# Triangular inversion of the gated delta rule: whole 128 x 128 weights in its products, and a new sequence of pieces

## The chip, the cores and the metric

The kernel runs on one core of a Trainium2 chip. The metric is the device time of one execution in microseconds (us). The engines are PE (TensorE), DVE (VectorE), ACT (ScalarE), POOL (GpSimd) and SP (SyncE, which issues the DMAs).

## The reference, cut to what matters

A two-layer encoder (512 tokens of width 1024). Each layer makes one wide projection; a differential attention with four heads and a gated delta rule with four heads, run in both directions, work on its parts; their results are gated, added and projected, and an MLP follows. The change touches the delta rule alone: the inverse of `eye + L`, where `L` is strictly lower triangular within chunks of 64 tokens. The kernel works it out in blocks of its own of 128 tokens.

```python
def gated_delta_rule_chunked(q, k, v, g, beta):
    ...
    L = jnp.where(strict, jnp.einsum('bhncd,bhnmd->bhncm', kb, k) * decay, 0.0)
    eye = jnp.eye(CHUNK, dtype=jnp.float32)
    T = lax.linalg.triangular_solve(eye + L, jnp.broadcast_to(eye, L.shape), left_side=True,
                                    lower=True, unit_diagonal=True)
    u = jnp.einsum('bhncm,bhnme->bhnce', T, v * beta[..., None])
    w = jnp.einsum('bhncm,bhnmd->bhncd', T, kb * jnp.exp(g)[..., None])
    ...
    def step(state, inp):
        ...
def reference(x, c, ada_w, ...):
    for l in range(DEPTH):
        ...
        proj = h @ w_in[l]
        ...
        y_a = diff_attention(...)
        y_b = gated_deltanet(...)
        ...
        x = x + gt1 * (merged @ w_out[l])
        h = rms_norm(x, norm2_g[l]) * (1.0 + sc2) + sh2
        x = x + gt2 * (jnp.square(jax.nn.relu(h @ w_mlp1[l])) @ w_mlp2[l])
    return x
```

## The kernel before

Python code first builds a list of operations, then a planner (`Plan.schedule`) sets the order in which every engine issues them, and `Plan.issue` (L431) emits them; so all rows of the profile name L431, and a group is known by its tiles. The planner is a list scheduler: it keeps a clock for every engine, gives each operation the time that `cost` (L451 and on) states, adds the lag between two engines from `LAG`, and takes at each step, of the operations that are ready, the one with the lowest key. The key is a level and the place in the program. `HOLD` lets a dense product wait for a moment when an operation of a more urgent level is about to be ready. Tiles come from pools of slots (F, Y, Z, and the eight PSUM banks B), and an operation can start only when its slot is free. Where the cost of an operation changes, the place of all later ones can change with it.

Dense products (`d_dn`, `d_da`, `d_z`, `d_g`, `d_out`, `d_m`) are done in a split form: each weight and each activation is a high part and a low part in the fp32r type (`whi`, `wlo`, `hh`, `hl`), and three products are added. ACT casts the high part of a weight, DVE subtracts to get the low part, and both come from a DMA.

`ORDER` (L490) is one string per layer and sets the order in which the pieces stand in the program: `q`, `k`, `v` are the projections of the attention, `d` the projection of a head of the delta rule (`d_dn`, with convolution and norm on DVE), `a` its first part (`kk`, `L`, `kq`, transposes `tokT` and `qT`), `b` the inversion of all 32 x 32 diagonal blocks at once on DVE (`gdn_b`, one batch for four heads), `z` a gate projection, `c` the rest of a head (`gdn_c`), and `t` a head of the attention. The digits are heads, or halves for `q`, `k` and `v`.

`gdn_c` (L1058 and on) joins the inverted diagonal blocks to the inverse of a whole 128 x 128 triangle, for four token tiles (`t`) and both directions (`d`). `four` issues four matmuls into one bank. First `pn` = `L` times the diagonal blocks, copied by ACT or DVE to `NTr`; then three products `px` = `NTr` times a part of `X`, one block diagonal after the other (`n` = 1, 2, 3), and each result is added or copied into `X` before the next one reads it. So `pn`, `px`, `px`, `px` of a direction are a serial chain through PE and ACT or DVE, and the serial recurrence over tokens (`pv`, `R`, `Vk`, `pS`) follows. In the kernel before, the stationary operand of a product has only the columns that the result needs: 128 or 96 for `pn` and for `n` = 1, 64 for `n` = 2 and 32 for `n` = 3. These operands are plain F32, and each such matmul stands in the profile as two instructions, each with its own weight load.

Of the kernel before, what the change touches and what calls it, by code (L numbers as in the profile page):

```python
# [17 lines left out]
P = 128  # L18
# [12 lines left out]
NB = 32  # L31
# [419 lines left out]
def cost(eng, fn, dst, ins, kw):  # L451
    n = int(np.prod(dst.shape[1:]))
    ptr = sum(isinstance(kw.get(k), View) for k in ("scalar", "scalar1", "scale", "bias"))
    psum = any(v.t.cls == "B" for v in ins)
    if ins:
        n = max([n] + [int(np.prod(v.shape[1:])) for v in ins]) if eng != "pe" else n
    if eng == "sp":
        return int(np.prod(dst.shape)) * 4 / 360.0
    if eng == "pe":
        if fn == "transpose":  # L460
            return 109.0
        if kw["lhsT"].dt == F32:
            return 4 * max(n, 32) / 2.4 + 9.0
        return 120.0 if n <= 256 else n / 2.4 + 14.0
    if eng == "act":
        return (51.0 if psum else 93.0) + 93.0 * ptr + n / 1.2 + (93.0 if kw.get("accum_out") is not None else 0.0)
    if eng == "dve":
        if fn == "memset":
            return 8.0 + n / 0.96
        if fn == "reciprocal":  # L470
            return 69.0 + 6.25 * n
        return 69.0 + 60.0 * ptr + n / 0.96
    if fn == "memset":
        return 36.0 + n / 1.2
    return 150.0 + (1.66 if any(v.a.strides[-1] == 0 for v in ins) else 2.1) * n
# [11 lines left out]
GS, NYF, KEEPM = (3, 5), 2, (3, 2)  # L487


ORDER = ("q0 d0 a0 d1 a1 d2 a2 d3 a3 b0 k0 z0 c0 z1 c1 k1 z2 q1 v0 t0 z3 t1 c3 c2 v1 t2 t3",  # L490
         "d0 q0 k0 d1 a1 d2 a0 a2 d3 a3 b0 z0 c0 z1 c1 k1 z2 c2 v0 t0 q1 z3 v1 c3 t2 t3 t1")


@with_exitstack
def encoder(ctx, tc, a, out):
# [3 lines left out]
    pe, act, dve, pool, sp = (Eng(pl, e) for e in ("pe", "act", "dve", "pool", "sp"))  # L499
    ad, dp = Eng(pl, "act", "dve"), Eng(pl, "dve", "pool")  # L500
# [126 lines left out]
    for i in range(2):  # L627
        half = slice(512 * i, 512 * i + 512)
        ps = B([P, 512], "cps")
# [143 lines left out]
    for l in range(DEPTH):  # L773
# [9 lines left out]
        for w in range(2):  # L783
            pool.tensor_tensor(out=cg[:, w], in0=ccos, in1=bc(gain[:, l, w], 1, NT), op=ALU.mult, after=[normed])
            pool.tensor_tensor(out=sg[:, w, :, 0:32], in0=csin[:, :, 0:32], in1=bc(gain[:, l, w, 32:64], 1, NT), op=ALU.mult,
                               after=[normed])
            pool.tensor_tensor(out=sg[:, w, :, 32:64], in0=csin[:, :, 32:64], in1=bc(gain[:, l, w, 0:32], 1, NT), op=ALU.mult,
                               after=[normed])
# [269 lines left out]
        def gdn_c(h, XA):  # L1058
# [16 lines left out]
            def four(name, lhsT, rhs, rows, cs):  # L1075
                ps = B([P, NT, P], name)
                for t in range(NT):
                    op = pe.matmul(ps[rows, t, cs], lhsT=lhsT[:, t], rhs=rhs[:, t], start=True, stop=True)
                return ps[rows, :, cs], op

            for d in range(2):
                NTr = Y([P, NT, P], "NT")
                if d == 0:
                    c1, full, ks = slice(0, P - NB), slice(0, P), slice(0, P)
                else:
                    c1, full, ks = slice(NB, P), slice(0, P - NB), slice(0, P - NB)
                    pool.memset(NTr[ks, :, 0:NB], 0.0, after=[gate["inv"]])
                ps, gate["pq"] = four("pn", L[:, d, :, full], DT[:, d, :, c1], full, c1)  # L1090
                ad.copy(NTr[full, :, c1], ps)
                for n in range(1, 4):
                    m = P - NB * n
                    rows, cs = (slice(0, m), slice(NB * n, P)) if d == 0 else (slice(0 if n == 1 else P - m, P), slice(0, m))
                    ps, op = four("px", NTr[ks, :, rows], X[ks, d, :, cs], rows, cs)
                    x = X[rows, d, :, cs]
                    if n == 1:
                        dve.tensor_tensor(out=x, in0=ps, in1=x, op=ALU.add)
                    else:
                        ad.copy(x, ps)  # L1100
# [453 lines left out]
```

## Time and profile before

| | us |
|---|---|
| median of 3 runs (1634.34 to 1637.26) | 1635.57 |
| profiled execution, its own time | 1637.45 |
| its span | 1635.7 |
| PE busy in the span | 1597.4 |
| DVE busy | 1314.3 |
| ACT busy | 829.7 |
| POOL busy | 164.9 |

The granted clock of the span is 0.99 of full speed. In the rows, PE is the matmul side of TensorE and PEld its weight load. A row of the timeline begins with its start and its duration; the name is result <- operands, then the shape of the weight (rows * columns), the shape of the result, and how many instructions in a row have this form. Matmuls are pipelined, so a row lasts longer than its distance to the next one: what an instruction costs is read from the distance between starts.

### The profile page before, as it was taken

To read this page: it belongs to the slowest core of one execution; us is meant where nothing else is said; L and a number is where in the kernel's file an instruction comes from. 1 tells how busy PE (TensorE), PEld (TensorE's weight loads), DVE (VectorE), ACT (ScalarE), POOL (GpSimd) and SP (SyncE) were. 2 spreads that over 40 slices of the span, in tenths; PEclk is the share of its full clock that TensorE was granted. 3 is DMA by queue.
4 is the path that set the end of the run, shared out by engine and by line. 5 is a ranking of instruction groups with operands and counts; after the bars stand their busy time and mean duration, and the time that the engine had idled before them with its cause. 6 is when DMAs were issued, how large, how long until landed. Compare 5 with 4: busy or idle time off the path is not lost.

```text
span 1635.7 us, 25251 instructions
## 1 busy us (share of the span) xinstructions
PE 1597.4 (98%) x9136; PEld 1385.3 (85%) x9136; DVE 1314.3 (80%) x2878; ACT 829.7 (51%) x1591; POOL 164.9 (10%) x170
## 2 busy tenths in 40 slices
PE   6989999999999999999989899999999999999998
PEld 5869988888899888888879799998888988888887
DVE  7999969899899988585998897699527885767676
ACT  4583335573266545454558442467423674636361
POOL 0253201000300000000005221000003000000000
PEclk9989999999999999999989999999999999999999
DMA  9423465538767483436233323422343525252542
GB/s 376 165 75 120 136 221 145 170 116 296 284 251 290 173 303 121 162 122 235 96 129 123 111 90 109 131 69 81 103 142 129 206 91 189 94 191 92 192 168 77
DMA packets 107726, 260.77 MB, mean 159 GB/s; under 512 B 27841, under 2 KB 40769, under 8 KB 107602
## 3 DMA queue, kind: packets, MB, share of 16 engines
q1 hardware_dynamic: 107602, 259.16, 46.1%
q8 instruction: 72, 1.18, 0.3%
q14 instruction: 52, 0.43, 0.1%
HBM read 242.31 MB, written 16.81 MB: 158 GB/s over the span
## 4 chain that ended last, share of the span: by engine, by line
PE 93%; DVE 4%; ACT 1%; issue 0%; DMA 0%; POOL 0%; SPq 0%; DVEq 0%; ACTq 0%
PE d_m L431 19%; PE d_g L431 11%; PE m2x L431 11%; PE d_da L431 8%; PE d_dn L431 6%; PE d_out L431 6%; PE m2y L431 5%; PE d_m1f L431 3%; PE d_z L431 3%; PE m2z L431 3%; PE d_brb L431 3%; PE d_bra L431 3%; PE sc L431 2%; PE px L431 2%; PE po L431 2%; PE pv L431 2%
## 5 line engine op out<-in xcount | busy, mean ns | idle before, releaser
L431 PE MATMUL d_m<-hh,whi_m 128*128 128x512 f32 x448 | 174.5, 389 | 0.0
L431 PE MATMUL d_m<-hl,whi_m 128*128 128x512 f32 x448 | 174.4, 389 | 0.0
L431 PE MATMUL d_m<-hh,wlo_m 128*128 128x512 f32 x448 | 174.4, 389 | 0.0
L431 DVE TENSOR_TENSOR m2lo<-m,m2hi 128x1024 fp32r<-128x1024 f32 x112 | 132.9, 1221 | 13.1 <-ACT m2hi L431 8.6
L431 ACT CAST m2hi<-m 128x1024 fp32r<-128x1024 f32 x112 | 114.8, 1048 | 50.1 <-DMA m<-in_w_m_dram 20.2
L431 DVE SCALAR_TENSOR_TENSOR ada<-ada,cb 128x1024 f32<-128x1024 f32 x96 | 116.5, 1227 | 2.6 <-DMA ada<-in_ada_w_dram 2.6
L431 PE MATMUL d_da<-whi_da,hh 128*128 128x256 f32 x384 | 109.4, 285 | 0.0
L431 PE MATMUL d_da<-whi_da,hl 128*128 128x256 f32 x384 | 109.1, 284 | 0.0
L431 PE MATMUL d_da<-wlo_da,hh 128*128 128x256 f32 x384 | 108.8, 285 | 0.0
L431 ACT ACTIVATE relu<-d_m 128x512 f32<-128x512 f32 x56 | 33.5, 598 | 147.8 <-PE d_m L431 147.8
L431 PE MATMUL d_g<-hh,wlo_g 128*128 128x512 f32 x256 | 102.0, 399 | 0.0
L431 PE MATMUL d_g<-hl,whi_g 128*128 128x512 f32 x256 | 102.0, 399 | 0.0
L431 PE MATMUL d_g<-hh,whi_g 128*128 128x512 f32 x256 | 102.0, 398 | 0.0
L431 PEld LDWEIGHTS d_m<-hh,wlo_m 128*128 128x128 f32 x448 | 84.1, 188 | 17.4
L431 PEld LDWEIGHTS d_m<-hh,whi_m 128*128 128x128 f32 x448 | 84.1, 188 | 17.4
L431 PEld LDWEIGHTS d_m<-hl,whi_m 128*128 128x128 f32 x448 | 84.1, 188 | 17.4
L431 PE MATMUL d_dn<-hh,whi_dn 128*128 128x512 f32 (+1 forms) x208 | 78.4, 387 | 2.6 <-DVE L L431 2.6
L431 PE MATMUL d_dn<-hh,wlo_dn 128*128 128x512 f32 (+1 forms) x208 | 79.3, 385 | 1.6 <-DVE wlo_dn L431 1.6
L431 DVE TENSOR_TENSOR u<-relu 128x256 f32<-128x256 f32 x64 | 27.1, 423 | 66.8 <-ACT relu L431 66.5
L431 PE MATMUL d_dn<-hl,whi_dn 128*128 128x512 f32 (+1 forms) x208 | 80.5, 387 | 0.0
L431 ACT CAST whi_m<-raw_m 128x1024 fp32r<-128x1024 f32 x56 | 58.7, 1049 | 42.3 <-DMA raw_m<-in_w_mlp_dram 35.7
L431 DVE TENSOR_TENSOR wlo_m<-raw_m,whi_m 128x1024 fp32r<-128x1024 f32 x56 | 67.9, 1221 | 12.6 <-ACT whi_m L431 12.4
(326 smaller groups left out, 4777.9 us busy)
## 6 DMA issues: line engine op xcount, KB each, us to landing
m<-in_w_m_dram SPq DMA_DIRECT2D x112, 512.0 KB, 4.3
ada<-in_ada_w_dram SPq DMA_DIRECT2D x96, 512.0 KB, 6.1
raw_m<-in_w_mlp_dram SPq DMA_DIRECT2D x56, 512.0 KB, 4.6
raw_g<-in_w_g_dram SPq DMA_DIRECT2D x32, 512.0 KB, 4.4
raw_out<-in_w_out_dram SPq DMA_DIRECT2D x32, 512.0 KB, 4.3
raw_dn<-in_w_dn_dram SPq DMA_DIRECT2D x24, 512.0 KB, 6.3
raw_da<-in_w_da_dram SPq DMA_DIRECT2D x24, 512.0 KB, 3.9
xs<-xT SPq DMA_DIRECT2D x24, 256.0 KB, 2.5
```

Of the source, the lines that this page charges most:

```text
L431: op.ins = getattr(eng[op.eng[0]], fn)(*[real(v) for v in op.args], **{k: real(v) for k, v in op.kw.items()})
```

## The change

Three things. First, in `gdn_c` all products of `pn` and `px` now take a whole 128 x 128 weight and write all 128 rows of their columns; the same rows as before are copied out of the bank. So that the unused columns of `NTr` are numbers, the 32 columns that `pn` doesn't write are set to zero for both directions and on all 128 rows, where before that was done on 96 rows and for one direction: eight POOL memsets more. The count of matmuls is the same; per layer and head, 4 `pn` go from 96 to 128 weight columns, 4 `px` with `n` = 1 likewise (the other 4 had 128 columns on 96 rows), 8 `px` go from 64 to 128, and 8 from 32 to 128. Second, `cost` gives an F32 matmul at least 111 ns times the share of the 128 result rows, where before at least that of 32 columns. Third, both strings of `ORDER` are new. The shape, the cost and the strings together move instructions all over the program.

```diff
@@ -460,7 +460,7 @@
         if fn == "transpose":
             return 109.0
         if kw["lhsT"].dt == F32:
-            return 4 * max(n, 32) / 2.4 + 9.0
+            return max(4 * n / 2.4 + 9.0, 111.0 * dst.shape[0] / P)
         return 120.0 if n <= 256 else n / 2.4 + 14.0
     if eng == "act":
         return (51.0 if psum else 93.0) + 93.0 * ptr + n / 1.2 + (93.0 if kw.get("accum_out") is not None else 0.0)
@@ -487,8 +487,8 @@
 GS, NYF, KEEPM = (3, 5), 2, (3, 2)
 
 
-ORDER = ("q0 d0 a0 d1 a1 d2 a2 d3 a3 b0 k0 z0 c0 z1 c1 k1 z2 q1 v0 t0 z3 t1 c3 c2 v1 t2 t3",
-         "d0 q0 k0 d1 a1 d2 a0 a2 d3 a3 b0 z0 c0 z1 c1 k1 z2 c2 v0 t0 q1 z3 v1 c3 t2 t3 t1")
+ORDER = ("q0 d0 a0 d1 d2 a1 a2 d3 a3 b0 k0 z0 c0 z1 c1 k1 q1 v0 z2 t0 z3 c2 t1 c3 v1 t2 t3",
+         "d0 q0 d1 k0 a1 d2 a0 a2 d3 a3 b0 z0 c0 z1 c1 v0 k1 z2 c2 t0 q1 v1 z3 t2 t3 t1 c3")
 
 
 @with_exitstack
@@ -1075,24 +1075,22 @@
             def four(name, lhsT, rhs, rows, cs):
                 ps = B([P, NT, P], name)
                 for t in range(NT):
-                    op = pe.matmul(ps[rows, t, cs], lhsT=lhsT[:, t], rhs=rhs[:, t], start=True, stop=True)
+                    op = pe.matmul(ps[:, t, cs], lhsT=lhsT[:, t], rhs=rhs[:, t], start=True, stop=True)
                 return ps[rows, :, cs], op
+
 
 
 
             for d in range(2):
                 NTr = Y([P, NT, P], "NT")
-                if d == 0:
-                    c1, full, ks = slice(0, P - NB), slice(0, P), slice(0, P)
-                else:
-                    c1, full, ks = slice(NB, P), slice(0, P - NB), slice(0, P - NB)
-                    pool.memset(NTr[ks, :, 0:NB], 0.0, after=[gate["inv"]])
-                ps, gate["pq"] = four("pn", L[:, d, :, full], DT[:, d, :, c1], full, c1)
-                ad.copy(NTr[full, :, c1], ps)
+                c1, c0 = (slice(0, P - NB), slice(P - NB, P)) if d == 0 else (slice(NB, P), slice(0, NB))
+                pool.memset(NTr[:, :, c0], 0.0, after=[gate["inv"]])
+                ps, gate["pq"] = four("pn", L[:, d], DT[:, d, :, c1], slice(0, P), c1)
+                ad.copy(NTr[:, :, c1], ps)
                 for n in range(1, 4):
                     m = P - NB * n
                     rows, cs = (slice(0, m), slice(NB * n, P)) if d == 0 else (slice(0 if n == 1 else P - m, P), slice(0, m))
-                    ps, op = four("px", NTr[ks, :, rows], X[ks, d, :, cs], rows, cs)
+                    ps, op = four("px", NTr, X[:, d, :, cs], rows, cs)
                     x = X[rows, d, :, cs]
                     if n == 1:
                         dve.tensor_tensor(out=x, in0=ps, in1=x, op=ALU.add)
```

In the projection stage of the second layer (`ORDER[1]`), PE's rows around the product `kk` of the head that comes first read like this before; `d_dn0`, `d_dn1` and `d_dn2` are the projections of a head's q, k and v, `kk` waits for the k of the head, normed on DVE:

```order
L431 MATMUL d_dn0_9714<-hl7_8915,whi_dn00_9424 128x512
L431 MATMUL d_dn0_9714<-hh7_8911,wlo_dn00_9431 128x512
L431 MATMUL d_dn2_9769<-hh0_8821,whi_dn20_9737 128x512
L431 MATMUL d_dn2_9769<-hl0_8828,whi_dn20_9737 128x512
L431 MATMUL d_dn1_9794<-hh0_8821,whi_dn10_9747 128x512
L431 MATMUL d_dn1_9794<-hl0_8828,whi_dn10_9747 128x512
L431 MATMUL kk_9808<-kqv1_9799 128x128 x4
L431 MATMUL tokT_9819<-cst_86,kqv1_9799 128x128 x4
L431 MATMUL d_dn0_9835<-hh0_8821,whi_dn00_9757 128x512
L431 MATMUL d_dn0_9835<-hl0_8828,whi_dn00_9757 128x512
L431 MATMUL d_dn2_9769<-hh0_8821,wlo_dn20_9829 128x512
L431 MATMUL d_dn2_9769<-hh1_8841,whi_dn20_9737 128x512
```

And now:

```order
L431 MATMUL d_da_9717<-wlo_da100_9433,hh1_8843 128x256
L431 MATMUL d_da_9717<-whi_da100_9424,hh2_8849 128x256
L431 MATMUL d_da_9717<-whi_da100_9424,hl2_8866 128x256
L431 MATMUL d_da_9717<-wlo_da100_9433,hh2_8849 128x256
L431 MATMUL kk_9746<-kqv1_9726 128x128 x3
L431 MATMUL qT_9753<-cst_86,kqv0_9732 128x128 x4
L431 MATMUL kk_9746<-kqv1_9726 128x128
L431 MATMUL kq_9763<-kqv0_9732,kqv1_9726 128x128 x4
L431 MATMUL tokT_9777<-cst_86,kqv1_9726 128x128 x4
L431 MATMUL d_da_9717<-whi_da100_9424,hh3_8872 128x256
L431 MATMUL d_da_9717<-whi_da100_9424,hl3_8881 128x256
L431 MATMUL d_da_9717<-wlo_da100_9433,hh3_8872 128x256
```

The projection `d_da` of the attention's k (`k0`) now stands ahead of `kk`, 49 matmuls in a row, where two starts of `d_dn` of the next head stood; the transposes `qkT` of the attention have left the place.

In `gdn_c` of the head that comes first in the first layer, PE's rows around the first chain read like this before (`px` with the results 96 x 96, 64 x 64 and 32 x 32 are direction 0, the next ones direction 1):

```order
L431 MATMUL px_2646<-X_2554,NT_2626 64x64 x4
L431 MATMUL d_z_2569<-hh5_399,whi_z0_2551 128x512
L431 MATMUL pn_2653<-DT_2423,L_1071 96x96 x3
L431 MATMUL px_2657<-X_2554,NT_2626 32x32 x4
L431 MATMUL pn_2653<-DT_2423,L_1071 96x96
L431 MATMUL d_z_2569<-hl5_406,whi_z0_2551 128x512
L431 MATMUL d_z_2569<-hh5_399,wlo_z0_2596 128x512
L431 MATMUL d_z_2569<-hh6_437,whi_z0_2551 128x512
L431 MATMUL pv_2672<-tok2_942,X_2554 128x128
L431 MATMUL px_2675<-X_2554,NT_2407 128x96 x4
L431 MATMUL d_z_2569<-hl6_446,whi_z0_2551 128x512
L431 MATMUL d_z_2569<-hh6_437,wlo_z0_2596 128x512
```

And now:

```order
L431 MATMUL d_z_2597<-hh7_485,wlo_z0_2592 128x512
L431 MATMUL px_2649<-X_2589,NT_2409 128x64 x4
L431 MATMUL pn_2656<-DT_2425,L_1072 128x96 x4
L431 MATMUL px_2662<-X_2589,NT_2409 128x32 x4
L431 MATMUL px_2678<-X_2589,NT_2412 128x96 x4
L431 MATMUL pv_2684<-tok2_940,X_2589 128x128
L431 MATMUL px_2690<-X_2589,NT_2412 128x64 x4
L431 MATMUL px_2699<-X_2589,NT_2412 128x32 x4
L431 MATMUL pv_2684<-tok2_940,X_2589 128x128
L431 MATMUL pn_2711<-DT_2665,L_1330 128x96
L431 MATMUL pS_2715<-Vk_2707,tok1_641 128x128
L431 MATMUL pn_2711<-DT_2665,L_1330 128x96
```

The gate's dense products `d_z`, which stood between the steps of the chain, are all issued before it reaches its second step; between these steps stand only products of the chain itself and of the recurrence after it, and the next dense product stands 54 rows after the last of them.

## Rows read from the trace of the kernel before

**Rows 1.** The page: busy us and share, and the chain that ended last.

```profile
PE 1597.4 (98%) x9136; PEld 1385.3 (85%) x9136; DVE 1314.3 (80%) x2878; ACT 829.7 (51%) x1591; POOL 164.9 (10%) x170
...
PE 93%; DVE 4%; ACT 1%; issue 0%; DMA 0%; POOL 0%; SPq 0%; DVEq 0%; ACTq 0%
```

**Rows 2.** Windows: stretch, busy us (instructions) by engine, clock, DMA share, GB/s.

```profile
108.00:125.00 17.00, 10.76 (x42) 7.96 (x41) 17.00 (x47) 6.91 (x24) 5.00 (x7) 0.61 0.26 75
896.00:916.00 20.00, 13.09 (x61) 10.85 (x60) 15.76 (x50) 9.57 (x26) 7.22 (x4) 0.83 0.29 84
1010.00:1110.00 100.00, 100.00 (x765) 89.23 (x764) 73.26 (x219) 50.49 (x139) 7.68 (x9) 1.00 0.38 101
```

**Rows 3.** Timeline of PE, blocks of eight F32 instructions between dense products.

```profile
212.98 0.40 PE L431 MATMUL d_z<-hh,whi_z 128*128 128x512 f32 x1
213.21 0.84 PE L431 MATMUL px<-X,NT 128*96 128x96 f32 x8
...
214.15 0.39 PE L431 MATMUL d_z<-hh,wlo_z 128*128 128x512 f32 x1
...
220.09 0.39 PE L431 MATMUL d_z<-hh,wlo_z 128*128 128x512 f32 x1
220.41 0.68 PE L431 MATMUL px<-X,NT 96*64 96x64 f32 x8
...
221.35 0.40 PE L431 MATMUL d_g<-hh,wlo_g 128*128 128x512 f32 x1
...
222.05 0.40 PE L431 MATMUL d_g<-hh,wlo_g 128*128 128x512 f32 x1
222.38 0.44 PE L431 MATMUL px<-X,NT 96*32 96x32 f32 x8
...
223.09 0.40 PE L431 MATMUL d_g<-hl,whi_g 128*128 128x512 f32 x1
...
247.24 0.40 PE L431 MATMUL d_z<-hl,whi_z 128*128 128x512 f32 x1
247.47 1.05 PE L431 MATMUL pog<-V,PT 128*128 128x128 f32 x8
...
248.59 0.60 PE L431 MATMUL pv<-R,X 128*128 128x128 f32 x4
```

**Rows 4.** Timeline of PE, 128 weight columns against 32 moving columns.

```profile
69.94 0.39 PE L431 MATMUL pg<-graw,ones 128*128 128x32 f32 x2
70.16 0.47 PE L431 MATMUL d_dn<-hl,whi_dn 128*128 128x512 f32 x1
```

**Rows 5.** Timeline of PEld, the weight loads of one narrow block.

```profile
220.41 0.54 PEld L431 LDWEIGHTS px<-X,NT 96*64 96x64 f32 x8 [0.36 <-issue]
```

**Rows 6.** Timeline of PE, the waits around the first `kk` of the second layer.

```profile
901.95 1.13 PE L431 MATMUL kk<-kqv 128*128 128x128 f32 x8 [3.65 <-DVE rqr L431]
...
905.58 0.50 PE L431 MATMUL d_dn<-hh,wlo_dn 128*128 128x512 f32 x1 [1.59 <-DVE wlo_dn L431]
...
908.22 0.69 PE L431 MATMUL qkT<-cst,rot 128*128 128x128 f32 x2 [1.67 <-POOL rot L431]
```

**Rows 7.** Timeline of PE, two neighbouring products of the attention's projection.

```profile
885.25 0.28 PE L431 MATMUL d_da<-whi_da,hh 128*128 128x256 f32 x1
885.37 0.28 PE L431 MATMUL d_da<-whi_da,hl 128*128 128x256 f32 x1
```

**Rows 8.** Timeline of PE, the head that comes first, first layer.

```profile
110.11 0.66 PE L431 MATMUL tokT<-cst,kqv 128*128 128x128 f32 x4 [1.74 <-DVE kqv L431]
...
116.48 0.77 PE L431 MATMUL d_dn<-hh,whi_dn 128*128 128x512 f32 x1 [2.61 <-DVE L L431]
...
119.55 1.12 PE L431 MATMUL qT<-cst,kqv 128*128 128x128 f32 x4 [1.87 <-DVE kqv L431]
...
122.03 0.79 PE L431 MATMUL d_dn<-hh,wlo_dn 128*128 128x512 f32 x1
```

**Rows 9.** Timeline of DVE and ACT, results of px going into X.

```profile
214.09 0.55 DVE L431 TENSOR_TENSOR X<-px,X 96x384 f32<-96x384 f32 x1 [0.91 <-PE px L431]
...
215.88 0.36 ACT L431 COPY X<-px 64x256 f32<-64x256 f32 x1 [2.95 <-PE px L431]
```

**Rows 10.** Groups by line, POOL: busy us, mean ns, idle before.

```profile
L431 POOL MEMSET NT<- 96x128 f32 x8 | 1.3, 199 | 0.0
```

## Prediction

> **What bounds the kernel now.** I read the page first: PE is busy in 98% of the span, and it holds 93% of the chain that ended last, DVE 4% [rows 1]. So a change in PE's work shows one for one, except in the few stretches where PE waits. The windows show where these are and where they are not. Between 108 and 125 us PE is busy for 10.76 of 17 us at a granted clock of 0.61, and DVE for all 17; between 896 and 916 us PE is busy for 13.09 of 20 at 0.83. Between 1010 and 1110 us, where the second layer's triangular products lie, PE is busy for 100 of 100 us at 1.00 [rows 2]. So the products that change stand, in the kernel before, in a full PE stream: what they cost is the distance between starts, and nothing hides it. The waits that a new sequence could remove are elsewhere, in the two projection stages.
>
> **Part 1: the whole weights, on PE.** The rows are read as the time from the start of the last dense product ahead of a block of eight instructions (four F32 matmuls) to the start of the second instruction group behind it, so that what a block does to its neighbours is inside. With 128 weight columns that is 248.59 - 247.24 = 1.35 us, with 96 columns 214.15 - 212.98 = 1.17, with 64 columns 221.35 - 220.09 = 1.26, with 32 columns 223.09 - 222.05 = 1.04 [rows 3]. The last three become the first. That the 128-column block has 128 moving columns and the new ones have 96, 64 or 32 makes no difference by the nearest row: two instructions with 128 weight columns against 32 moving ones take 70.16 - 69.94 = 0.22 us, so 0.11 each [rows 4], and the block of eight takes 1.35 less two dense steps of 0.23 (247.47 - 247.24), or 0.89, again 0.11 each [rows 3]. The weight sets the pace, not what moves.
>
> A whole weight therefore costs 0.18 us a block more than 96 columns, 0.09 more than 64, and 0.31 more than 32. The 64-column step is that small because a narrow block pays at its edge: it starts 0.32 us after the dense product ahead of it where the others start 0.23 after [rows 3], and its weight load sits 0.36 us idle before it begins, with no releaser that the profile shows [rows 5]. Per layer and head, direction 0 has one block each of the three kinds (0.58 us); direction 1 has its `pn` with 96 columns, its first `px` already with 128, then one of 64 and one of 32 (0.58 us). Two layers of four heads: 8 x 1.16 = **+9.3 us**. The lower bound is 8.8: the starts are rounded to 0.01, and 48 blocks changed by 0.01 each make 0.5. The upper one is 12.2: some narrow blocks of the kernel before stand next to each other and save the 0.09 at the edge, 32 x 0.09 = 2.9 if all did. I take 9.3, since most have other work between them.
>
> The Trainium skill, page "TensorEngine Tiling (Array Packing)", section "Key Properties", says that a change of the tiling mode drains TensorE. This speaks for the change, as whole weights need no other mode; the 0.36 us of idle weight load agrees with it. By the page alone one would book 32 such drains of 0.36 us as a gain, 11.5 us, and come out at -2.2 us for this part instead of +9.3; the starts in the rows already contain what of them reaches PE's pace.
>
> **Part 2: copies, memsets and the planner's price.** The copies out of PSUM have as many elements in a row as before, so I book nothing. Eight more memsets of about 0.2 us each are 1.6 us on POOL [rows 10], which is busy for 10% [rows 1]; the zeros need no result of the chain, so they lie beside dense work. If that cover were gone, each would hold up one chain by 0.2 us. The new price in `cost` does nothing on the chip but move instructions; that is part 3.
>
> **Part 3: the sequence.** Three places matter.
>
> First, the chain of the first layer. A result of `px` goes to X by DVE in 0.55 us or by ACT in 0.36 [rows 9]. DVE began 0.26 us after the last of the eight starts (213.21 + 7 x 0.089 = 213.83 against 214.09; 0.089 is the 96-column block's 1.17 less 0.46, by eight) [rows 3, 9]. Taking the same 0.26 for the way back, an estimate, the next step of a chain can start 1.07 us (DVE) or 0.88 us (ACT) after that last start, where PE would have gone on after 0.11: 0.96 or 0.77 us of wait. With other work to issue this costs nothing, and before it was there. In the new order the chains of the head that comes first (its direction 1) and of the next head run through 54 rows of PE without a dense product. Step by step, less the work that stands between at 0.11 us an instruction: direction 1 of the first head 0.96 - 0.22 (two instructions of `pv`), 0.77, and 0.5 behind the shortest copy; direction 0 of the next head 0.96 - 0.45 (four instructions) and 0.1 (six); its direction 1 0.96 - 0.45 and 0.77. Together **+3.9 us** of new waits. Bounds: 0 if the recurrence between them happens to fill every gap, and 7 if the recurrence's own steps wait as well. The second half of that layer and the second layer interleave two to four chains, and I book 0 to 1 there.
>
> Second, the start of the second layer's heads. PE waits 3.65 us for DVE's `rqr` ahead of `kk`, 1.59 for the low part of a weight and 1.67 for `rot` [rows 6], 6.9 us in all, and at a clock of 0.83 over 20 us it loses another 3.4 [rows 2]. The new `ORDER[1]` has the k projection of the attention ahead of it: 49 products in a row stand before `kk`, at 0.12 us each [rows 7] 5.9 us. That is more than the longest wait, and may keep the clock up. But the low part of the next weight, which these products need too, comes from DVE, which is busy for 15.76 of the 20 us [rows 2]; in the new order only its high part is used ahead of `kk`, so the planner itself sees it late, and two more waits of 2 us or so remain. I take half of the 10.3 us, **-5 us**; bounds 0 and -10.3.
>
> Third, the start of the first layer's heads. There PE waits 1.74, 2.61 and 1.87 us and takes up its dense stream at 122.03 [rows 8]. DVE is busy in every microsecond [rows 2]. The new `ORDER[0]` lets `d2` go before `a1`, which gives PE other rows to wait with, but the weight's low part, the convolution and `L` are all DVE's, and none gets shorter. What is late next is the same low part. I book **0**, with one such wait either way, -1.9 to +1.9.
>
> **The sum.** 9.3 + 3.9 - 5 + 0 = +8.2 us. The profiled execution took 1637.45 us and would take 1645.6; it is 1.9 above the median, so on the median it is 1635.57 + 8.2 = **1643.8 us**.
>
> **The rivals.** (a) The new sequence pays back the weights: the second layer's waits and slow clock go altogether (-10.3) and the first layer's chain finds its work (0 to +2). That gives -1 to +1, 1635 to 1637. For it: 5.9 us of work against a wait of 3.65. Against it: DVE's 15.76 of 20. (b) Faster: the first layer's start is freed as well. It has 6.2 us of waits and 17 x 0.39 = 6.6 us of clock [rows 2, 8], 12.8 us; with half of that and all of the second layer's the sum is 9.3 + 2 - 10.3 - 6.4 = -5.4, 1630. It decides from the point where the two starts together give back more than the 13.2 us of the weights and the chain; against it stands DVE's full 17 of 17, which no order of PE shortens. (c) Slower still: the 54 rows starve PE so far that the granted clock falls as it did at 108 us. Seventeen microseconds at 0.61 would be 6.6 us more: 1650.4. For it, that gaps of 1.7 to 2.6 us were enough there; against it, that mine are below 1 us each. (d) The page's rule on drains, as a mechanism here: if PE gave back the whole idle 0.36 us of each of the 32 narrow blocks, and my block of 128 columns were no guide, the sum would be -2.2 + 3.9 - 5 = -3.3, 1632.3. The starts in rows 3 speak against it directly.
>
> **How the numbers follow.** Forecast (both effects of the order roughly cancel, the weights remain): 0.61, with 1639 to 1650. (a) 0.15, (b) 0.11, (c) 0.10, (d) 0.03. The range reaches down to 1633, which leaves out (b) and (d), and up to 1652, beyond (c)'s 1650.4, so some 0.17 lies outside. About 0.2%, or 3.3 us, is what a measurement of this kernel can tell from no change: slower is the forecast and (c), 0.71; the same is (a) and a little of (d), 0.16; faster is (b) and the rest of (d), 0.13.
>
> **What would show it.** All `pn` and `px` rows should have 128*128 weights and starts 0.11 us apart, the idle load ahead of the narrow blocks should be gone, and PE's busy time should grow by about 9 us with its idle time still near the 38.3 us of before (the span's 1635.7 less 1597.4 [rows 1]). In the first layer's chain PE rows should show waits of 0.1 to 0.8 us for DVE and ACT, some seven of them. Around the second layer's first `kk` the wait should be below 2 us with a clock of nearly 1.00. It is wrong if starts of the new blocks lie below 0.10 us, if the first layer's start gives back over 4 us, or if the chain's waits don't appear.

## The result, and the profile after

The changed kernel takes 1649.2 us in the median of 4 runs (1649.0 to 1649.61), against 1636.41 for the kernel before, now over 4 runs (1634.34 to 1637.84): a ratio of 1.0079, 95% interval 1.0062 to 1.0097, so 12.8 us slower (10 to 16). The forecast was slower, 1643.8 us, with a range from 1633 to 1652. The profiled execution took 1649.0 us, 11.6 more than that of before, with a span of 1646.9 us.

The page of the kernel after, busy us by engine and the chain that ended last, to be laid beside [rows 1]:

```profile
PE 1606.7 (98%) x9136; PEld 1401.0 (85%) x9136; DVE 1314.7 (80%) x2884; ACT 827.5 (50%) x1585; POOL 160.6 (10%) x178
...
PE 90%; DVE 5%; ACT 3%; DMA 1%; issue 1%; SPq 0%; DVEq 0%; ACTq 0%
```

PE is busy 9.3 us longer (1606.7 - 1597.4), and idle 40.2 us of the span against 38.3. So on the face of it the loss is work and not waiting. But the stretches tell more. These are windows of the kernel after (stretch, busy us and instructions of PE, PEld, DVE, ACT and POOL, granted clock, DMA share, GB/s). The first, third and fourth answer to [rows 2], the last two of them shifted by the 11 us by which the second layer starts later:

```profile
108.00:125.00 17.00, 10.86 (x55) 8.67 (x54) 17.00 (x49) 7.70 (x25) 4.70 (x7) 0.80 0.25 72
205.00:245.00 40.00, 36.23 (x244) 32.91 (x244) 23.72 (x50) 11.60 (x28) 1.59 (x4) 0.91 0.50 165
907.00:927.00 20.00, 17.63 (x123) 15.99 (x124) 19.93 (x47) 11.19 (x29) 5.13 (x4) 1.00 0.26 100
1021.00:1121.00 100.00, 100.00 (x719) 92.35 (x718) 67.89 (x202) 45.57 (x122) 5.16 (x7) 1.00 0.36 95
```

The chains of the second layer are as full as before. The start of the second layer's heads has 17.63 us of PE work in 20 at full clock, where it had 13.09 at 0.83. The start of the first layer's heads has 10.86 us of work in 17, where it had 10.76, at a clock of 0.80 in place of 0.61. And a new hole has come: between 205 and 245 us PE works for 36.23 of 40 us, at 0.91. That stretch of the kernel before was full:

```profile
205.00:245.00 40.00, 40.00 (x291) 34.03 (x290) 26.37 (x53) 11.94 (x29) 1.58 (x3) 1.00 0.66 218
```

PE's timeline there in the kernel after (start, duration, operation, count, and in brackets the idle time before it with what ended it). The first three rows answer to the 96-column block of [rows 3]:

```profile
213.31 0.40 PE L431 MATMUL d_z<-hh,whi_z 128*128 128x512 f32 x1
213.54 1.03 PE L431 MATMUL px<-X,NT 128*128 128x96 f32 x8
...
214.67 0.40 PE L431 MATMUL d_z<-hh,wlo_z 128*128 128x512 f32 x1
...
217.35 1.95 PE L431 MATMUL px<-X,NT 128*128 128x32 f32 x16
219.14 0.41 PE L431 MATMUL pv<-tok,X 128*128 128x128 f32 x2
219.95 1.10 PE L431 MATMUL px<-X,NT 128*128 128x64 f32 x8 [0.40 <-DVE X L431]
221.56 1.08 PE L431 MATMUL px<-X,NT 128*128 128x32 f32 x8 [0.50 <-ACT X L431]
223.04 0.80 PE L431 MATMUL pv<-tok,X 128*128 128x128 f32 x2 [0.40 <-ACT X L431]
```

All weights are 128*128. From the dense start at 213.31 to the second dense start behind the block, 214.67, are 1.36 us, where the 96-column block took 1.17. Sixteen instructions with 32 moving columns take 219.14 - 217.35 = 1.79 us, 0.11 each. And from 219.95 on each step of the chain waits 0.4 to 0.5 us for the copy of the step before, while no dense product is there to be issued. The clock falls with it (windows of the kernel after):

```profile
222.00:225.00 3.00, 2.53 (x13) 2.17 (x13) 1.31 (x5) 0.74 (x3) 0.00 (x0) 0.61 0.37 89
225.00:230.00 5.00, 4.97 (x26) 4.78 (x24) 1.78 (x6) 0.62 (x2) 0.00 (x0) 0.55 0.61 222
```

Two waits of that stretch are not the chain's: 0.92 us at 207.72 for the low part of a gate's weight, and 0.68 us at 211.65 for a DMA. The chain's own waits are 0.40, 0.50 and 0.40 us above, and 0.19 and 0.50 us further on, 2.0 us in all:

```profile
207.72 0.50 PE L431 MATMUL d_z<-hh,wlo_z 128*128 128x512 f32 x1 [0.92 <-DVE wlo_z L431]
...
211.65 1.10 PE L431 MATMUL pn<-DT,L 128*128 128x96 f32 x8 [0.68 <-DMA DT<-scrT]
...
237.31 0.63 PE L431 MATMUL px<-X,NT 128*128 128x32 f32 x4 [0.50 <-ACT X L431]
```

The start of the second layer's heads, to be laid beside [rows 6], and that of the first layer's, beside [rows 8], both PE in the kernel after:

```profile
907.15 0.38 PE L431 MATMUL d_da<-whi_da,hh 128*128 128x256 f32 x1 [1.84 <-ACT whi_da L431]
...
911.80 0.91 PE L431 MATMUL kk<-kqv 128*128 128x128 f32 x6 [1.40 <-DVE kqv L431]
...
917.47 0.39 PE L431 MATMUL d_da<-wlo_da,hh 128*128 128x256 f32 x1 [0.48 <-DVE wlo_da L431]
```

```profile
112.18 1.16 PE L431 MATMUL kk<-kqv 128*128 128x128 f32 x8 [2.08 <-DVE kqv L431]
...
117.50 1.12 PE L431 MATMUL qT<-cst,kqv 128*128 128x128 f32 x4 [3.55 <-DVE kqv L431]
...
121.33 0.50 PE L431 MATMUL d_dn<-hh,wlo_dn 128*128 128x512 f32 x1 [0.51 <-DVE wlo_dn L431]
```

In the second layer 6.9 us of waits have become 1.84 + 1.40 + 0.34 + 0.48 = 4.1. In the first, three waits with 6.2 us in all have become 2.08 + 3.55 + 0.51 = 6.1.

To add idle time and slow clock without counting either twice, I took, for every PE instruction of the trace, what its distance to the next start exceeds the usual distance for its kind between the same neighbours at full clock. Summed by stretch, before and after: 100 to 130 us, 11.2 and 9.2; 205 to 245 us, 0.4 and 7.8; 895 to 930 us, 10.2 and 5.0; the other stretches together change by less than 0.5. These changes are -2.0, +7.4 and -5.2, with the rest +0.1, so waits and clock come out nearly even. What is left of the 11.2 us between the spans, some 10.9, is put down to the longer distance of the `px` and `pn` instructions themselves. It is a remainder and holds what the usual distances miss: a direct reading in the next section gives 9.7.

### The profile page after: what moved, and what is told of

Same layout as the page of the kernel before. It is cut to its first block, busy times and chain, and to the rows that moved or that the text cites. A ratio compares the mean times of both kernels' runs of the same rounds, so it can differ in the third digit from the quotient of the medians.

```text
span 1646.9 us, 25267 instructions
## 1 busy us (share of the span) xinstructions
PE 1606.7 (98%) x9136; PEld 1401.0 (85%) x9136; DVE 1314.7 (80%) x2884; ACT 827.5 (50%) x1585; POOL 160.6 (10%) x178
## 4 chain that ended last, share of the span: by engine, by line
PE 90%; DVE 5%; ACT 3%; DMA 1%; issue 1%; SPq 0%; DVEq 0%; ACTq 0%
PE d_m L431 19%; PE m2x L431 11%; PE d_g L431 11%; PE d_da L431 8%; PE d_out L431 6%; PE m2y L431 5%; PE d_dn L431 5%; PE d_m1f L431 3%; PE m2z L431 3%; PE d_brb L431 3%; PE d_bra L431 3%; PE px L431 3%; PE d_z L431 2%; PE sc L431 2%; PE po L431 2%; ACT w L431 2%
## 5 line engine op out<-in xcount | busy, mean ns | idle before, releaser
L431 PE MATMUL d_m<-hh,whi_m 128*128 128x512 f32 x448 | 174.3, 389 | 0.0
L431 PE MATMUL d_m<-hl,whi_m 128*128 128x512 f32 x448 | 174.3, 389 | 0.0
L431 PE MATMUL d_m<-hh,wlo_m 128*128 128x512 f32 x448 | 174.3, 389 | 0.0
L431 DVE TENSOR_TENSOR m2lo<-m,m2hi 128x1024 fp32r<-128x1024 f32 x112 | 133.0, 1221 | 13.3 <-ACT m2hi L431 8.8
L431 ACT CAST m2hi<-m 128x1024 fp32r<-128x1024 f32 x112 | 114.8, 1047 | 51.1 <-DMA m<-in_w_m_dram 19.0
L431 DVE SCALAR_TENSOR_TENSOR ada<-ada,cb 128x1024 f32<-128x1024 f32 x96 | 116.7, 1228 | 5.8 <-DMA ada<-in_ada_w_dram 5.7
L431 PE MATMUL d_da<-whi_da,hh 128*128 128x256 f32 x384 | 108.9, 285 | 1.8 <-ACT whi_da L431 1.8
L431 PE MATMUL d_da<-whi_da,hl 128*128 128x256 f32 x384 | 109.0, 285 | 0.0
L431 PE MATMUL d_da<-wlo_da,hh 128*128 128x256 f32 x384 | 108.2, 284 | 0.5 <-DVE wlo_da L431 0.5
L431 ACT ACTIVATE relu<-d_m 128x512 f32<-128x512 f32 x56 | 33.5, 598 | 148.4 <-PE d_m L431 148.4
L431 PE MATMUL d_g<-hh,whi_g 128*128 128x512 f32 x256 | 101.9, 398 | 0.0
L431 PE MATMUL d_g<-hl,whi_g 128*128 128x512 f32 x256 | 101.6, 397 | 0.0
L431 PE MATMUL d_g<-hh,wlo_g 128*128 128x512 f32 x256 | 101.0, 395 | 0.0
L431 PEld LDWEIGHTS d_m<-hh,whi_m 128*128 128x128 f32 x448 | 84.1, 188 | 17.5
L431 PEld LDWEIGHTS d_m<-hh,wlo_m 128*128 128x128 f32 x448 | 84.1, 188 | 17.5
L431 PEld LDWEIGHTS d_m<-hl,whi_m 128*128 128x128 f32 x448 | 84.1, 188 | 17.3
L431 ACT CAST whi_m<-raw_m 128x1024 fp32r<-128x1024 f32 x56 | 58.7, 1049 | 41.5 <-DMA raw_m<-in_w_mlp_dram 36.8
L431 PE MATMUL d_dn<-hl,whi_dn 128*128 128x512 f32 (+1 forms) x208 | 79.4, 382 | 0.0
L431 DVE TENSOR_TENSOR u<-relu 128x256 f32<-128x256 f32 x64 | 27.1, 423 | 65.5 <-ACT relu L431 65.3
L431 PE MATMUL d_dn<-hh,wlo_dn 128*128 128x512 f32 (+1 forms) x208 | 78.5, 380 | 0.5 <-DVE wlo_dn L431 0.5
L431 DVE TENSOR_TENSOR wlo_m<-raw_m,whi_m 128x1024 fp32r<-128x1024 f32 x56 | 68.0, 1221 | 13.5 <-ACT whi_m L431 13.2
L431 PE MATMUL d_dn<-hh,whi_dn 128*128 128x512 f32 (+1 forms) x208 | 77.4, 382 | 0.5 <-ACT sqj L431 0.5
```

The lines of the kernel that those rows point to most:

```text
L431: op.ins = getattr(eng[op.eng[0]], fn)(*[real(v) for v in op.args], **{k: real(v) for k, v in op.kw.items()})
```

## The experiments

The kernels are named by their labels. Where a kernel keeps a sequence "instruction for instruction", the planner worked on the shapes of one kernel, and the operands of the other were put in as the instructions were issued. A line number of 433 or 435 in their rows is that of the same helper, L431.

**The two halves of the change apart.** `w_all` is the kernel before, planned as it was, with whole weights put in at issue:

```diff
-  planned and issued: matmul(ps[rows, t, cs], lhsT=NTr[ks, t, rows], rhs=X[ks, d, t, cs])
+  planned as above, issued: matmul(ps[:, t, cs], lhsT=NTr[:, t], rhs=X[:, d, t, cs])
   (pn, its copy and the memsets of NT likewise; direction 0's memset right ahead of its copy)
```

> The sequence of the kernel before, instruction for instruction on PE, ACT, DVE and SP, with all pn and px products at whole 128 x 128 weights (eight POOL memsets more). Theory A (a whole F32 weight takes 0.11 us an instruction, and that is all that the weights do): 9.3 us by the blocks of the trace of before, up to 11 where narrow blocks stood next to each other, so 1645.7 to 1647.4 us. Rival B (the weights cost little, the new sequence makes the whole loss): 1636 to 1638 us. Rival C (leaving the narrow tiles gives back the idle 0.36 us of weight load at 32 blocks): 1632 to 1635 us.

Measured: 1645.79 us, ratio 1.0051 (1.0038 to 1.0063), so 6.2 to 10.3 us more. `n_after` is the reverse, the kernel after in its own sequence with the narrow weights of before:

```diff
-  issued: matmul(ps[:, t, cs], lhsT=NTr[:, t], rhs=X[:, d, t, cs])
+  planned as above, issued: matmul(ps[rows, t, cs], lhsT=NTr[ks, t, rows], rhs=X[ks, d, t, cs])
```

> The sequence of the kernel after, instruction for instruction, with the narrow weights of before issued in it (copies of pn's second direction 96 rows long again; the memsets stay). Theory A: the sequence's gains and losses nearly cancel (-2.0 at 108 us, +7.4 in the first layer's chains, -5.3 at 898 us, -0.7 in the second layer's chains), so 1635 to 1639 us. The chains' waits may grow, since narrow products leave more time open. Rival B: 1646 to 1649 us, as the kernel after.

Measured: 1639.6 us, ratio 1.0018 (1.0009 to 1.0027), 1.5 to 4.4 us more. That is 0.6 us above the range of theory A. The two add to the whole within their intervals: some 8 to 9 us belong to the weights, some 3 to the sequence. Rival B and rival C fall. The weights can also be read directly, as each pair of kernels has one and the same sequence on PE. From the instruction ahead of a run of changed instructions to the second one behind it, all such runs together take 9.1 us longer in `w_all` than in the kernel before, and 9.7 longer in the kernel after than in `n_after`. The holes in the chain stand in the narrow kernel too (PE of `n_after`):

```profile
221.50 0.44 PE L433 MATMUL px<-X,NT 96*32 96x32 f32 x8 [0.50 <-ACT X L433]
222.34 0.80 PE L433 MATMUL pv<-tok,X 128*128 128x128 f32 x2 [0.40 <-ACT X L433]
```

So it is not the width that starves it.

**Which string starves or saves.** `e3` is the kernel after with the old first string, `e10` the kernel before with the new second string:

```diff
 e3:  -ORDER[0] of after      +ORDER[0] of before
 e10: -ORDER[1] of before     +ORDER[1] of after
```

> The kernel after with the first string of ORDER put back (whole weights, new cost, second string new). If the first string makes the starved chains of the first layer (+7.4) and the gain at 108 us (-2.0): 1642 to 1645 us. If the chains starve by the whole weights and the new cost, whatever the string: 1649 to 1652 us.

Measured: 1666.93 us, ratio 1.0186 (1.0172 to 1.02). Both expectations missed, by some 15 us and more. The stretch of the chains is far worse with the old string (window of `e3`):

```profile
205.00:245.00 40.00, 30.12 (x123) 26.54 (x122) 17.07 (x37) 5.51 (x14) 1.06 (x2) 0.56 0.42 146
```

123 PE instructions in 40 us, at a clock of 0.56, where the kernel before issues 291. So the new first string doesn't starve the chains, it repairs most of what something else in the change does to them.

> The kernel before with the second string of ORDER alone taken from the kernel after (narrow weights, old cost, first string old). If the 5.3 us at the start of the second layer's heads come from that string alone and nothing later takes them back: 1630 to 1632 us. If the gain needs the new prices of the planner, or a later wait takes it back: 1635 to 1637 us.

Measured: 1635.77 us, ratio 0.9991 (0.9982 to 1.0), so 0 to 3 us gained. The waits of that stretch, in PE's timeline, and its window, some 11 us earlier than in the kernel after:

```profile
896.45 0.38 PE L431 MATMUL d_da<-whi_da,hh 128*128 128x256 f32 x1 [1.83 <-ACT whi_da L431]
...
907.19 0.54 PE L431 MATMUL d_da<-wlo_da,hh 128*128 128x256 f32 x1 [2.05 <-DVE wlo_da L431]
```

```profile
890.00:910.00 20.00, 16.13 (x103) 15.21 (x102) 17.01 (x31) 14.01 (x37) 6.27 (x8) 0.85 0.42 139
```

The 6.9 us of waits are down to 3.9, for a weight's high part and its low part, but the clock is still below full. The second string by itself brings part of the 5 us.

**What starves the chains.** Four things were left: the weights as planned, the price, the strings, and the four memsets a layer that had been booked at nothing. `bmem` adds those to the kernel before, and nothing else:

```diff
+                if d == 0:
+                    pool.memset(NTr[:, :, P - NB:P], 0.0, after=[gate["inv"]])
                 ps, gate["pq"] = four("pn", ...)
```

> The kernel before with one thing of the change: the four POOL memsets per layer that clear NT's unused columns of direction 0 (128 rows x 128 elements) are among the planned operations. Weights, price and strings are old. Theory D (these memsets, through the planner, take the dense products away from between the steps of the first layer's chains): waits of 0.4 to 0.8 us at 210 to 245 us and a half clock there, 1645 to 1665 us. Rival (the memsets are hidden on POOL and harmless; the whole weights, the price or the strings starve the chains): 1635 to 1639 us.

Measured: 1670.39 us, ratio 1.0212 (1.0198 to 1.0226): 35 us for eight memsets of 0.2 us, above even the range of theory D. The window of the chains, and PE's timeline in it:

```profile
205.00:245.00 40.00, 28.60 (x142) 24.16 (x141) 19.96 (x43) 6.55 (x17) 1.57 (x3) 0.62 0.47 155
```

```profile
212.70 2.00 PE L431 MATMUL pn<-DT,L 128*128 128x96 f32 x8 [4.04 <-DMA DT<-scrT]
...
224.02 0.87 PE L431 MATMUL px<-X,NT 96*64 96x64 f32 x8 [1.29 <-DVE X L431]
```

PE stands 4.04 us before the first `pn`, for the DMA that brings the diagonal blocks, and then before many of the steps, at a clock of 0.62 in the mean: 28.60 us of work, and 142 instructions where the kernel before issues 291. In the second layer it stands once more, before a dense product ahead of the chains:

```profile
1038.55 0.80 PE L431 MATMUL d_z<-hh,wlo_z 128*128 128x512 f32 x1 [7.13 <-DVE wlo_z L431]
```

No memset ends any of these waits. POOL's 1.57 us in the window are as many as in the kernel before. What the memsets do, they do in the plan.

`amem` takes them out of the plan of the kernel after and issues each right ahead of the copy into its tile:

```diff
-                pool.memset(NTr[:, :, c0], 0.0, after=[gate["inv"]])
+                if d:
+                    pool.memset(NTr[:, :, c0], 0.0, after=[gate["inv"]])
   (direction 0: issued ahead of ad.copy(NTr[:, :, c1], ps), not planned)
```

> The kernel after with direction 0's memsets taken out of the plan: each is issued on POOL right ahead of the copy into the same NT tile; all the rest of the change stands. Theory D: the 7.4 us of waits and slow clock between 205 and 245 us go, 1641 to 1644 us. Rival (the strings, the price or the whole weights starve the chains): 1647 to 1651 us.

Measured: 1642.04 us, ratio 1.0038 (1.0025 to 1.005), 7.2 us below the kernel after between the medians, 6.7 by the two ratios. The hole is closed (window of `amem`):

```profile
205.00:245.00 40.00, 39.67 (x276) 36.05 (x274) 24.25 (x48) 10.22 (x24) 2.60 (x7) 1.00 0.50 160
```

`bmemlate` is `bmem` with the memsets tied to a later operation:

```diff
-                    pool.memset(NTr[:, :, P - NB:P], 0.0, after=[gate["inv"]])
+                    pool.memset(NTr[:, :, P - NB:P], 0.0, after=[gate[("tr", 0)]])
   (gate[("tr", 0)]: the transpose of the head's own diagonal blocks)
```

> The kernel before with the same four memsets per layer among the planned operations, but each made to wait for its own head's transposed diagonal blocks, so that the NT tile is claimed when the head's chain begins and not when the inversion batch ends. If the early claim is what made the 35 us: 1634 to 1638 us, no waits in the chains. If the memset as such does it (POOL's time, a wait of PE or of the copy for POOL): 1650 us or more.

Measured: 1636.13 us, ratio 1.0001 (0.9992 to 1.001), and the window from 205 to 245 us is full:

```profile
205.00:245.00 40.00, 40.00 (x290) 34.26 (x290) 26.79 (x54) 11.30 (x26) 1.73 (x4) 1.00 0.63 204
```

The same memsets in the plan cost 35 us or nothing, by when they may go. `gate["inv"]` is an operation in the middle of the inversion batch that serves all four heads, so all of them become ready together, and each claims its head's tile NT in the Y pool (58 slots) long before the chain needs it. POOL's rows show it: in `bmem` all eight memsets of the first layer, old and new, are done by 193 us, while in `bmemlate` the new ones come one by one, at 204, 220, 296 and 329 us. Of `bmem` the last two, of `bmemlate` the first of the new ones:

```profile
192.53 0.34 POOL L431 MEMSET NT<- 128x128 f32 x2
```

```profile
204.15 0.21 POOL L431 MEMSET NT<- 128x128 f32 x1
```

The dense products of the gates that fill the chains, `d_g` and `d_z`, are not used up earlier, they come later. Between 190 and 205 us PE issues 33 of them in the kernel before and 33 in `bmem`; between 205 and 245 us 85 and 17. The windows of `d_g` and then `d_z` alone, in the kernel before (busy us and instructions of PE and PEld first):

```profile
205.00:245.00 40.00, 17.80 (x61) 10.30 (x60) 0.58 (x1) 1.00 0.66 218
205.00:245.00 40.00, 7.35 (x24) 4.15 (x24) 0.69 (x1) 0.59 (x1) 1.00 0.66 218
```

And in `bmem`:

```profile
205.00:245.00 40.00, 0.00 (x0) 0.00 (x0) 0.00 (x0) 0.62 0.47 155
205.00:245.00 40.00, 3.66 (x17) 2.70 (x15) 0.00 (x0) 0.43 (x1) 0.62 0.47 155
```

That the early claims hold these products back is argued from the code: the result of a gate product takes a slot of the same pool too (`sg`, `zg`), and gets it only while a reserve of slots stays free. What is shown is that the moment decides, and that the dense products are late.

**The price.** `b_newcost` is the kernel before with the new line in `cost` alone.

```diff
-            return 4 * max(n, 32) / 2.4 + 9.0
+            return max(4 * n / 2.4 + 9.0, 111.0 * dst.shape[0] / P)
```

> The kernel before with the new price in cost alone (old strings, narrow weights, no memsets more). It moves instructions and changes none. If the price by itself is neutral, as the sum took it: 1633 to 1639 us. If it is part of what starves the chains: 1640 us or more, with waits at 205 to 245 us.

Measured: 1641.29 us, ratio 1.0035 (1.0021 to 1.0048), 3.4 to 7.9 us more. Not neutral, and not by starved chains either: from 205 to 245 us PE is busy for 39.24 of 40 us. One new wait is plain, in PE's timeline at a later chain:

```profile
284.52 0.58 PE L431 MATMUL pn<-DT,L 128*96 128x96 f32 x4 [1.35 <-DVE DT L431]
```

It accounts for 1.35 us. The rest is spread over the sequence and stays open.

**The width by itself.** `w_32` puts whole weights into the products of n = 3 alone, in the sequence of the kernel before (as `w_all`, for `m == 32`).

> The sequence of the kernel before, with only the products of n = 3 (32 weight columns) made whole. By the blocks of the trace 16 blocks x 0.31 us = +5.0, 1641 to 1642.5 us, more than half of what all sizes together gave. Rival (each block loses the same, whatever its size, since the drain at a narrow block's edge pays for its width): a third of the 8 to 9 us, 1639 to 1640 us.

Measured: 1641.9 us, ratio 1.0037 (1.0025 to 1.005), 4.1 to 8.2 us, 6.5 between the medians. The rows of PE, the same place as the 32-column block of [rows 3]:

```profile
222.88 0.39 PE L435 MATMUL d_g<-hh,wlo_g 128*128 128x512 f32 x1
223.12 0.97 PE L435 MATMUL px<-X,NT 96*128 96x32 f32 x8
...
224.24 0.39 PE L435 MATMUL d_g<-hl,whi_g 128*128 128x512 f32 x1
```

1.36 us in place of 1.04, as worked out. At direction 0 the block stands here between the instructions of a `pn`, in the kernel before and in `w_32`:

```profile
216.11 0.67 PE L431 MATMUL pn<-DT,L 128*96 128x96 f32 x6
216.71 0.44 PE L431 MATMUL px<-X,NT 128*32 128x32 f32 x8
...
217.27 0.48 PE L431 MATMUL d_z<-hl,whi_z 128*128 128x512 f32 x1
```

```profile
216.59 0.67 PE L435 MATMUL pn<-DT,L 128*96 128x96 f32 x6
217.09 1.00 PE L435 MATMUL px<-X,NT 128*128 128x32 f32 x8
...
218.10 0.47 PE L435 MATMUL d_z<-hl,whi_z 128*128 128x512 f32 x1
```

From the `pn` ahead to the dense product behind it took 217.27 - 216.11 = 1.16 us and takes 1.51, 0.35 more. That is nearly the price of a block between dense products. Over all 16 blocks of the two traces, which have the same sequence on PE, the distances grow by 4.8 us, near the +5.0 of the expectation; the interval of the medians, 4.1 to 8.2, holds it, and whether the 1.7 us between 4.8 and 6.5 are noise stays open.

`c72` goes the other way with direction 0: 72 weight columns in place of 64 and 32, in the sequence of before.

```diff
-  issued: matmul(ps[rows, t, cs], lhsT=NTr[:, t, rows], ...)    rows = 0:64 (n = 2), 0:32 (n = 3)
+  issued: matmul(ps[0:72, t, cs], lhsT=NTr[:, t, 0:72], ...)
```

> The sequence of the kernel before, with direction 0's products of n = 2 and n = 3 at 72 weight columns in place of 64 and 32 (the rest narrow as before). If the narrow blocks' edges are a matter of the tile width of 64 and 32, as the Trainium skill's drain rule has it, and 72 columns run in the mode of 128 at some 0.07 us an instruction: n = 2 saves 0.8 - 0.55 = 0.25 us a block, n = 3 some 0.05, 8 x 0.3 = 2.4 us, 1633 to 1634 us, and blocks of 0.55 us between dense products. If the edges stay whatever the width: 8 x 0.34 = 2.7 us more, 1638 us.

Measured: 1633.32 us, ratio 0.9984 (0.9975 to 0.9993), 1.1 to 4.1 us less. PE's timeline:

```profile
214.78 0.40 PE L435 MATMUL d_z<-hh,wlo_z 128*128 128x512 f32 x1
215.02 0.67 PE L435 MATMUL px<-X,NT 128*72 128x64 f32 x8
...
215.82 0.67 PE L435 MATMUL pn<-DT,L 128*96 128x96 f32 x6
216.32 0.65 PE L435 MATMUL px<-X,NT 128*72 128x32 f32 x8
...
216.98 0.48 PE L435 MATMUL d_z<-hl,whi_z 128*128 128x512 f32 x1
```

The block of n = 2 begins 0.24 us after the dense product, and the next group starts 215.82 - 214.78 = 1.04 us after it, where the 64-column block with fewer columns took 1.26 [rows 3]. The block of n = 3 behind it takes 216.98 - 215.82 = 1.16 us with 72 columns, as much as above with 32. So the edge belongs to the tile widths of 64 and 32. The Trainium skill says on the page "TensorEngine Tiling (Array Packing)", "Key Properties", that a change of the tiling mode drains TensorE. The rows here agree with that, and put the price of the 64-column edge at no less than 1.26 - 1.04 = 0.22 us a block: 0.32 - 0.24 = 0.08 before it begins, and 0.94 - 0.80 = 0.14 from its start to the second start behind. That is not the 0.36 us of idle weight load [rows 5].

**A version below both.** `e2a` keeps the narrow weights and the memsets of before, takes both new strings, and prices all `pn` and `px` at 111 ns in the plan.

```diff
-            return 4 * max(n, 32) / 2.4 + 9.0
+            if dst.t.name.split("_")[0] in ("pn", "px"):
+                return max(4 * n / 2.4 + 9.0, 111.0)
+            return max(4 * n / 2.4 + 9.0, 111.0 * dst.shape[0] / P)
   (and both strings of ORDER as in the kernel after)
```

> The kernel before, narrow weights and its own memsets, with both new strings and with all pn and px priced at 111 ns. Theory D: without the eight memsets the new strings keep their gains (-2 at 108 us, -5 at 898 us) and don't starve the chains: 1629 to 1634 us, below both kernels. Rival (the strings themselves starve the chains, as in the kernel with the after's sequence and narrow weights): 1638 to 1641 us.

Measured: 1632.78 us, ratio 0.998 (0.9971 to 0.9989). `best72` adds the 72 columns to it.

> The narrow kernel with both new strings and without direction 0's memsets, as measured at 1632.8 us, with direction 0's n = 2 and n = 3 at 72 columns. If both gains add: 1629.5 to 1631.5 us. If the 72 columns bring nothing: 1632 to 1634 us.

Measured: 1630.85 us, ratio 0.9965 (0.9952 to 0.9977), 4 to 8 us below the kernel before and 18 below the kernel after. Both gains add.

## Why the prediction was right, and where it was not

**The weights (part 1).** Predicted +9.3, bounds 8.8 to 12.2. Alone, in the sequence of before, they cost 6.2 to 10.3 us; read directly they are 9.1 there and 9.7 in the kernel after. The price of a block was right to 0.01 us at the 96- and 32-column blocks, and a block between the instructions of a `pn` loses about as much as one between dense products (0.35 us against 0.32), so it mattered little that many narrow blocks don't stand between dense products.

**The memsets and the price (part 2).** "The zeros need no result of the chain, so they lie beside dense work" is true of their time on POOL and false of the kernel: this is the step that failed. In a kernel whose planner works with claimed slots, an operation that costs nothing on its engine can cost 35 us. With the rest of the change around it, it costs some 7 us (kernel after less `amem`). The new price in `cost`, also booked at nothing, is worth 3 to 8 us by itself in the old sequence.

**The chains (part 3, first).** Predicted +3.9 of new waits, with bounds 0 to 7; measured +7.4, above the upper bound. The place was right, and it could be read from the order that the planner gave, whatever had made it: the rows from 219.95 on show the waits one after the other. But they are five and not some seven, and each of the first three is shorter than worked out, 0.40, 0.50 and 0.40 us for 0.74, 0.77 and 0.5: the chain's own waits make 2.0 us. That the idle time of the stretch, 40 - 36.23 = 3.8 us, is so near to the 3.9 is luck, since 1.6 us of it are the waits for a weight's low part and for a DMA that the sum did not have. What the term lacked besides is the clock, 0.91 over the 40 us, which is 3.6 us. Rival (c) named that mechanism, and "against it, that mine are below 1 us each" was the wrong reason: behind gaps of 0.4 to 0.5 us between small products it fell, and the two instructions of `pv` at 223.04 last 0.80 us where they lasted 0.41 at 219.14. Whether the two longer waits at 207 to 212 us had a part in it isn't shown.

**The second layer's start.** Predicted -5, measured -5.2. The mechanism is the one described: the k projection fills the wait, and a high and a low part of a weight (1.84 and 0.48 us) and the normed k (1.40) stay as waits. The split was another than half of each: the clock came back whole, at 1.00, and of the 6.9 us of waits 2.8 went, so that the size came out this well is partly luck.

**The first layer's start.** Predicted 0, bounds -1.9 to +1.9; measured -2.0, just past the bound, all of it clock. The idle time is 6.1 us after 6.2. DVE is busy in all 17 us as before, as the prediction had it. The clock there need not be the change's doing: `w_all` and `c72`, with the sequence of before, show 0.80 in the same window where the profiled execution of before showed 0.61 [rows 2]. The window of `w_all`:

```profile
108.00:125.00 17.00, 9.31 (x42) 6.78 (x40) 17.00 (x48) 7.34 (x25) 5.02 (x7) 0.80 0.24 63
```

**The rivals.** (a) and (b) needed the sequence to give back the weights; it gave back 7 us (5.2 and 2.0) and took 7.4. (c) came halfway. (d) falls with `w_all` and `w_32`: whole weights cost more than narrow ones even where a narrow block's drain is saved.

Term by term, the sum of +8.2 became the +11.2 between the two spans by +0.4 in the weights as read directly, +3.5 in the chains, -0.2 in the second layer's start, -2.0 in the first layer's, +0.1 elsewhere, and 1.2 us that no reading assigns. The medians lie 12.8 apart, 1.6 more than the two spans, within the interval of the ratio. So direction and range held, with the weights as the main term; the term of the chains came out at nearly twice its size, for a reason that the sum had booked at nothing.

## What to carry to other kernels

An operation that is free on its engine isn't free in a plan: look at which tile it holds and from when, and tie it to the moment at which that tile is needed. Read the new order for places where a serial chain has lost the independent work between its steps, and price these with the slow clock and not with the gaps alone. In these F32 products the columns of the weight set the pace (0.11 us an instruction at 128 columns, with 96 moving columns as with 32), so widen a weight only up to where a narrow tile's edge costs more than the columns.

## What the runs showed of the hardware

A block of four F32 matmuls with 72 weight columns is quicker than one with 64 (1.04 us against 1.26 from the dense start ahead to the second start behind it), and no slower than one with 32 (1.16 us against 1.16 from the `pn` ahead to the dense product behind): blocks of 64 and 32 columns pay at their edges, 64 columns 0.08 us before the block begins and 0.14 from there on. Behind waits of no more than 0.5 us each in a chain of small products, with waits of 0.92 and 0.68 us some 10 us earlier, the granted clock fell to 0.61 and 0.55 between 222 and 230 us, so for most of that time to its lower level, 1.2 GHz; 0.91 over the 40 us around it is some 7 us at half, an estimate. And the length of a slow stretch differs between executions of one sequence: 0.61 and 0.80 over the same 17 us at the first layer's start.
